# Last products of a half projection and first weights of the gated unit, reordered in a two-layer decoder trunk

## The chip, the core and the metric

The kernel runs on one core of a Trainium2 chip. The metric is the time of one execution on the device in microseconds (us): the median of several runs. The engines are named as in the profile: PE is TensorE (matrix products), DVE is VectorE, ACT is ScalarE, POOL is GpSimd, and SP is SyncE, whose queue issues the DMA transfers.

## What is computed

Two layers over 1024 tokens of width 1024, in float32: an attention layer, then a state-space (S5) layer whose output is gated. Cut to the part that the change touches (the second layer, `h` being the normed input):

```python
proj = h @ w_in                                   # 1024 x 2048
u, z = proj[..., :1024], proj[..., 1024:]
y = s5_scan(u, ...)                               # per group of 16 channels
g = gelu(y)
y = g * sigmoid(g @ w_glu + b_glu)                # the gated unit
x = x + rms_norm((y * silu(z)) @ w_out, post_norm)
```

## The kernel before

**Products.** Every float32 matrix is split in two reduced-precision parts, a high part (the cast) and a low part (what the cast left out), so that one product becomes three: high weights with high input, high weights with low input, low weights with high input. `proj_half` (L119) makes one *half projection*: 128 output channels for 512 tokens, which is 8 steps k of 128 input channels, 3 products each, 24 products of 128x512 into one PSUM bank. `proj_part` (L107) issues them, k by k, in the order hi·hi, hi·lo, lo·hi, so that the low part of the weights is wanted by the third product.

**Weights.** `load_w` (L95) fetches one 128x1024 block of weights by DMA from SP (L100, tile `wraw`), ACT casts it (L88, `whi`), and DVE subtracts (L89, `wlo`). The pools of all three have two buffers, so the load of block e+2 waits until block e is split, and the split of block e+2 until PE is done with block e.

**The second layer.** `layer1` runs 16 blocks of `ssm_w_in` through `in_order` (L774), each for both token halves (th 0 and 1). The first 8 give `u`, the last 8 give `z` (L1463 on ACT, L1464 on DVE, stored to `z_dr`). Between these projections the state-space work for 8 groups of channels runs: products `py` on PE (L1433, L1434), a gelu that goes ACT L1435 and L1436, POOL L1437 and L1438, ACT L1439, DVE L1440, and a store of the rows `Y` to DRAM (`y_dr`, L1441), in two halves per group.

**The gated unit.** `glu` (L1494) reads `y_dr` back transposed (SP L1506, tile `gy`, six half-tile slots in a ring), for th 0 and 1 and for 8 k each, and splits each piece: ACT casts it (L88, `g0b` for th 0, `g1b` for th 1) and DVE takes the low part (L89). A slot is refilled when its piece has been split. `in_order` with `start="block"` then runs the first four half projections (two blocks of weights, two token halves; PSUM tiles `psb`) together: first k 0 to 6 of all four, then the four triples of k 7, whose input comes last from the last group. After these, blocks 2 to 7 follow one half after the other (`psj`). The output projection (`pso`, weights `wf0h`, `wf1b`) stands behind.

**The order.** Each engine runs its own instructions strictly in the order in which a scheduler has put them when the kernel is built; the scheduler estimates times of its own, and `high_priority` (in `load_w`) and `issue_after` shift what it picks. An instruction that waits holds up all that stands behind it on its engine.

Of the kernel before, what the change touches and what calls it, by code (L numbers as in the profile page):

```python
# [23 lines left out]
P = 128  # L24
S = 1024
D = 1024
KT = 8
# [18 lines left out]
def f32(ap):  # L46
    return ap.bitcast(F32)
# [36 lines left out]
def split(c, hi, lo, src, scale=None, engine=None):  # L84

    nc = c.nc
    if scale is None:
        c.last_hi = nc.scalar.copy(hi, src).ins  # L88
        return (engine or nc.vector).tensor_tensor(lo, src, f32(hi), op=ALU.subtract)  # L89
    else:  # L90
        nc.scalar.activation(hi, src, AF.Copy, scale=scale)
        nc.vector.scalar_tensor_tensor(lo, src, scale, f32(hi), op0=ALU.mult, op1=ALU.subtract)


def load_w(c, src):  # L95

    nc = c.nc
    with c.tc.high_priority(AHEAD):
        raw = c.wraw.tile([P, KT * P], F32, tag="wraw", name="wraw")
        nc.sync.dma_start(raw, src)  # L100
        hi = c.wsp.tile([P, KT * P], F32R, tag="whi", name="whi")
        lo = c.wsp.tile([P, KT * P], F32R, tag="wlo", name="wlo")
        c.last_lo = split(c, hi, lo, raw, engine=c.w_engine).ins
    return hi, lo


def proj_part(c, ps, w, h, ks, first=True):  # L107

    nc = c.nc
    wh, wl = w  # L110
    hh, hl = h
    for k in ks:
        s = slice(k * P, k * P + P)
        for n, (a, b) in enumerate(((wh, hh), (wh, hl), (wl, hh))):
            nc.tensor.matmul(ps, a[:, s], b[:, k, :], start=first and k == 0 and n == 0,  # L115
                             stop=k == KT - 1 and n == 2, skip_group_check=True)


def proj_half(c, w, h):  # L119
# [861 lines left out]
def post_weight(c, src):  # L981

    t = c.outs.tile([P, D], F32, tag="O", name="post", bufs=4)
    c.nc.sync.dma_start(t, bass.AP(src.tensor, src.offset, [[0, P], [1, D]]))
    return t
# [458 lines left out]
def y_view(c, et, th):  # L1444

    return bass.AP(c.y_dr.tensor, c.y_dr.offset + et * P * S + th * 4 * 16384, [[P, P], [16384, 4], [1, P]])
# [44 lines left out]
    return groups[7].load_U.ins  # L1491


def glu(c, a, last_input):  # L1494
    nc, tc = c.nc, c.tc
    bh = c.cst.tile([P, KT], F32, name="bh")
    nc.sync.dma_start(bh, a["b_glu"])
    nc.vector.tensor_scalar(bh, bh, 0.5, None, op0=ALU.mult)
    g, y2 = [], []
    ring = [x[:, n * H:n * H + H] for x in (c.outs.tile([P, D], F32, tag="O", name="gy", bufs=4) for _ in range(3)) for n in range(2)]  # L1500
    for th, tags in enumerate((("b1", "b4"), ("b5", "b3"))):
        g.append([c.pb.tile([P, KT, H], F32R, tag=t, name=f"g{th}{t}") for t in tags])
        for et in range(8):
            y = ring[(8 * th + et) % 6]
            with tc.issue_after(last_input):
                nc.sync.dma_start(y.rearrange("p (i n) -> p i n", i=4), y_view(c, et, th))  # L1506
            split(c, g[th][0][:, et, :], g[th][1][:, et, :], y)
    y2.append([c.pb.tile([P, KT, H], F32R, tag=t, name=f"y0{t}") for t in ("b0", "b2")])

    def use(eo, th, ps):  # L1510
        if th == 1 and len(y2) == 1:
            y2.append([c.pa2.tile([P, KT, H], F32R, tag=t, name=f"y1{t}") for t in ("y1h", "y1l")])
        t, z, y = c.slot("tg"), c.slot("zg"), c.slot("yg")
        nc.sync.dma_start(z, c.z_dr[eo, :, th * H:th * H + H])
        nc.sync.dma_start(y.rearrange("p (i n) -> p i n", i=4), y_view(c, eo, th))
        nc.gpsimd.tensor_tensor(z, z, y, op=ALU.mult)
        with tc.high_priority(AHEAD):
            nc.scalar.activation(t, ps, AF.Tanh, scale=0.5, bias=bh[:, eo:eo + 1])
            nc.vector.scalar_tensor_tensor(z, t, 1.0, z, op0=ALU.add, op1=ALU.mult)
            split(c, y2[th][0][:, eo, :], y2[th][1][:, eo, :], z, 0.25)  # L1520

    in_order(c, [a["w_glu"][e] for e in range(8)], g, use, start="block")
    return y2


def trunk(tc, a):
    c = Ctx()
    nc = tc.nc
    c.nc, c.tc = nc, tc
    c.turn = 0  # L1530

    c.banks, c.wide = 0, 0
    with ExitStack() as es:
        pool = lambda name, **k: es.enter_context(tc.tile_pool(name=name, **k))
        c.cst = pool("cst", bufs=1)
        c.small = pool("small", bufs=3)
        c.wraw = pool("wraw", bufs=2)
        c.wsp = pool("wsp", bufs=2)
        c.ring = pool("ring", bufs=1)
        c.outs = pool("outs", bufs=1)  # L1540
        c.psj = pool("psj", bufs=2, space=PSUM)
        c.pst = pool("pst", bufs=2, space=PSUM)
        c.pso = pool("pso", bufs=2, space=PSUM)

        c.es_ps = es.enter_context(ExitStack())
        c.ps = lambda name, bufs: c.es_ps.enter_context(tc.tile_pool(name=name, bufs=bufs, space=PSUM, reuse_waits="tile"))
        c.psl = c.ps("psl", 2)
        c.dr = pool("dr", bufs=1, space=DRAM)
        dram = lambda name, shape: c.dr.tile(shape, F32, name=name)
        c.vec_dr = dram("vec_dr", [3, 16, 384])  # L1550
        c.v_dr = dram("v_dr", [3, 2, S, H])
        c.ms_dr = dram("ms_dr", [8, 3, 4, S])
        c.wt_dr = dram("wt_dr", [8, 3, 2, S])
        c.on_dr = dram("on_dr", [8, P, S])
        c.x1_dr = dram("x1_dr", [8, P, D])
        c.g_dr = dram("g_dr", [8, P, S])
        c.u_dr = dram("u_dr", [8, P, S])
        c.y_dr = dram("y_dr", [8, P, S])
        c.z_dr = dram("z_dr", [8, P, S])
        c.k_dr = dram("k_dr", [64, 16, 240])  # L1560
        c.ca_dr = dram("ca_dr", [8, P, 1152])
        c.bt_dr = dram("bt_dr", [8, P, S])
        c.tab_dr = dram("tab_dr", [P, S + H])
        c.rot_dr = dram("rot_dr", [8, 3, 64, S])
        c.identr = c.cst.tile([P, P], F32R, name="identr")
        c.ident = f32(c.identr)
        tabs = c.cst.tile([P, 11, 2, 32], F32, name="tabs")
        pairs = [(tabs[:, k, 0, :], tabs[:, k, 1, :]) for k in range(11)]
        c.apow, c.bfac, c.rot = pairs[0:3], pairs[3], pairs[4:11]
        c.rho = c.cst.tile([P, 64], F32, name="rho")  # L1570
        c.dsk = c.cst.tile([P, 8], F32, name="dsk")

        c.es_pa = es.enter_context(ExitStack())
        c.pa = c.es_pa.enter_context(tc.tile_pool(name="pa", bufs=1, side="left"))
        c.es_attn = es.enter_context(ExitStack())
        h = attention(c, a)
        c.es_attn.close()
        c.es_ps.close()
        c.psl = c.ps("psl2", 2)
        c.pb = es.enter_context(tc.tile_pool(name="pb", bufs=1, side="right", reuse_waits="tile"))  # L1580
        g, raw = attn_gate(c, a, h)
        z112 = c.outs.tile([P, D], F32, tag="O", name="z112", bufs=4)[:, 0:8 * 112]
        nc.gpsimd.memset(z112, 0.0)
        nc.sync.dma_start(bass.AP(c.k_dr.tensor, c.k_dr.offset, [[8 * 240, P], [240, 8], [1, 112]]),
                          z112.rearrange("p (k x) -> p k x", k=8))
        h1, ws = attn_out(c, a, g, raw)
        c.es_pa.close()
        last_input = layer1(c, a, h1, ws)
        c.es_pa.close()
        c.pa2 = c.es_pa.enter_context(tc.tile_pool(name="pa2", bufs=1, side="left", reuse_waits="tile"))  # L1590
        y2 = glu(c, a, last_input)

        w = [[c.pa2.tile([P, KT, H], F32R, tag=f"w0{x}", name=f"wf0{x}") for x in "hl"],
             [c.pb.tile([P, KT, H], F32R, tag=t, name=f"wf1{t}") for t in ("b1", "b4")]]
        for n in range(2):
            for k in range(KT):
                rw = c.wraw.tile([P, H], F32, tag="wraw", name="wfr")
                nc.sync.dma_start(rw, a["ssm_w_out"][k, :, n * H:n * H + H])
                split(c, w[n][0][:, k, :], w[n][1][:, k, :], rw)
        post = post_weight(c, a["ssm_post_norm"])  # L1600
        ov = a["out"].rearrange("(n i) d -> i n d", i=8)
        out_tiles(c, y2, w, post, lambda i: c.x1_dr[i], lambda i, x: nc.sync.dma_start(ov[i], x), K_ORDER, 1,
                  lambda x, ns: nc.sync.dma_start(ov[7][:, ns], x[:, ns]))
# [90 lines left out]
```

## Time and profile before

| what | before |
|---|---|
| time, median of 3 runs (lowest to highest) | 1668.17 us (1667.24 to 1670.62) |
| the profiled execution, its time | 1668.29 us |
| the profiled execution, its span | 1666.5 us |
| PE busy | 1640.4 us, 98% |
| DVE, ACT, POOL busy | 1020.5, 709.6, 469.7 us |

The span counts from the first instruction to the last; some 1.8 us of the measured time lie around it. PE is the engine to read: where it is busy without a break at its full clock, other engines can only matter by keeping it so. The table of waits shows which of its idle stretches were ended by what, the timeline gives the single instructions, and PEclk (1.00 is 2.4 GHz, 0.50 is 1.2 GHz) tells how fast a busy PE ran.

### The profile page before, as it was taken

To read this page: it belongs to the slowest core of one execution; us is meant where nothing else is said; L and a number is where in the kernel's file an instruction comes from. 1 tells how busy PE (TensorE), PEld (TensorE's weight loads), DVE (VectorE), ACT (ScalarE), POOL (GpSimd) and SP (SyncE) were. 2 spreads that over 40 slices of the span, in tenths; PEclk is the share of its full clock that TensorE was granted. 3 is DMA by queue.
4 is the path that set the end of the run, shared out by engine and by line. 5 is a ranking of instruction groups with operands and counts; after the bars stand their busy time and mean duration, and the time that the engine had idled before them with its cause. 6 is when DMAs were issued, how large, how long until landed. Compare 5 with 4: busy or idle time off the path is not lost.

```text
span 1666.5 us, 26394 instructions
## 1 busy us (share of the span) xinstructions
PE 1640.4 (98%) x9746; PEld 1389.8 (83%) x9746; DVE 1020.5 (61%) x2513; ACT 709.6 (43%) x1732; POOL 469.7 (28%) x303
## 2 busy tenths in 40 slices
PE   7999999999999999999999999999999999899998
PEld 5889999988888888888888888888888888777886
DVE  8698898725455454545545454557563799945533
ACT  5232222326556454655646464555353232334411
POOL 2000010141342522434252243503320455522121
PEclk8999999999999999999999999999999999999999
DMA  6223455441232323323232332416336888574522
GB/s 227 87 50 108 154 170 175 136 146 55 70 102 72 110 74 91 93 72 99 72 109 87 92 105 76 133 52 192 125 115 206 246 247 239 170 225 156 167 103 87
DMA packets 176858, 212.21 MB, mean 127 GB/s; under 512 B 37443, under 2 KB 133462, under 8 KB 176728
## 3 DMA queue, kind: packets, MB, share of 16 engines
q1 hardware_dynamic: 176728, 210.52, 42.0%
q8 instruction: 77, 1.26, 0.3%
q14 instruction: 53, 0.43, 0.1%
HBM read 153.51 MB, written 56.96 MB: 126 GB/s over the span
## 4 chain that ended last, share of the span: by engine, by line
PE 88%; DVE 6%; DMA 3%; issue 1%; POOL 1%; ACT 1%; SPq 0%; DVEq 0%; ACTq 0%; POOLq 0%
PE psj L115 47%; PE psq L378 10%; PE psl L476 5%; PE pso L553 4%; PE pt L504 4%; PE pso L897 3%; PE pso L899 3%; PE pso L898 3%; PE pso L579 1%; PE psb L115 1%; PE psv L239 1%; PE psv L238 1%; DVE wlo L89 1%; PE psv L237 1%; DVE T L1414 1%
## 5 line engine op out<-in xcount | busy, mean ns | idle before, releaser
L115 PE MATMUL psj<-hh,wlo 128*128 128x512 f32 x896 | 358.3, 400 | 0.0
L115 PE MATMUL psj<-hh,whi 128*128 128x512 f32 x896 | 358.2, 400 | 0.0
L115 PE MATMUL psj<-hl,whi 128*128 128x512 f32 x896 | 354.9, 396 | 0.0
L89 POOL TENSOR_TENSOR wlo<-wraw,whi 128x1024 fp32r<-128x1024 f32 x48 | 115.3, 2402 | 392.6 <-ACT whi L88 347.3
L115 PEld LDWEIGHTS psj<-hh,whi 128*128 128x128 f32 x896 | 168.9, 188 | 36.6
L115 PEld LDWEIGHTS psj<-hh,wlo 128*128 128x128 f32 x896 | 168.8, 188 | 36.5
L115 PEld LDWEIGHTS psj<-hl,whi 128*128 128x128 f32 x896 | 168.9, 188 | 36.0
L493 ACT ACTIVATE lg<-lg,nm 128x128 f32<-128x128 f32 (+1 forms) x384 | 168.2, 443 | 35.5 <-DVE nm L488 35.5
L482 DVE CUSTOM_DVE_ANT_0 lg<-psl,T 128x128 f32<-128x128 f32 (+1 forms) x384 | 110.6, 347 | 90.4 <-PE psl L476 90.4
L88 ACT CAST whi<-wraw 128x1024 fp32r<-128x1024 f32 x80 | 83.7, 1046 | 131.9 <-PE psj L115 87.1
L378 PE MATMUL psq<-whi,v 128*128 128x256 f32 x640 | 115.6, 280 | 0.0
L115 PE MATMUL psj<-h1h,wlo 128*128 128x512 f32 (+1 forms) x272 | 103.9, 383 | 4.6 <-DVE wlo L89 4.6
L89 DVE TENSOR_TENSOR ph<-pt,ph 128x512 fp32r<-128x512 f32 (+2 forms) x160 | 96.7, 622 | 15.6 <-ACT ph L88 13.5
L89 DVE TENSOR_TENSOR kl<-psj,kh 128x512 fp32r<-128x512 f32 x48 | 33.2, 692 | 117.8 <-ACT kh L88 117.3
L115 PE MATMUL psj<-h1h,whi 128*128 128x512 f32 (+1 forms) x272 | 105.2, 387 | 0.0
L115 PE MATMUL psj<-h1l,whi 128*128 128x512 f32 (+1 forms) x272 | 103.0, 379 | 0.2 <-DVE h1l L89 0.2
L88 ACT CAST ph<-pt 128x512 fp32r<-128x512 f32 (+2 forms) x160 | 81.6, 530 | 46.3 <-PE pt L504 45.3
L378 PEld LDWEIGHTS psq<-whi,v 128*128 128x128 f32 x640 | 98.4, 188 | 1.2 <-ACT whi L88 0.6
L378 PE MATMUL psq<-wlo,v 128*128 128x256 f32 x320 | 89.8, 281 | 1.2 <-DVE wlo L89 1.2
L553 PE MATMUL pso<-ph,vs 128*128 128x256 f32 (+1 forms) x544 | 86.5, 284 | 0.0
L1277 POOL TENSOR_TENSOR Ks<-Ks,O 128x16 f32<-128x16 f32 x8 | 4.0, 498 | 285.4 <-ACT Ks L1275 285.4
L504 PE MATMUL pt<-identr,lg 128*128 128x128 f32 x560 | 82.2, 276 | 0.0
(288 smaller groups left out, 3719.6 us busy)
## 6 DMA issues: line engine op xcount, KB each, us to landing
wraw<-in_w_in_dram SPq DMA_DIRECT2D x56, 512.0 KB
mw<-wt_dr SPq DMA_DIRECT2D x48, 256.0 KB
v<-in_w_v_dram SPq DMA_DIRECT2D x20, 512.0 KB
vp<-v_dr SPq DMA_DIRECT2D x16, 512.0 KB
wraw<-in_ssm_w_in_dram SPq DMA_DIRECT2D x16, 512.0 KB
v_dr<-v SPq DMA_DIRECT2D x30, 256.0 KB
rot_dr<-rt SPq DMA_DIRECT2D x48, 128.0 KB
ca_dr<-ca SPq DMA_DIRECT2D x32, 144.0 KB
```

Of the source, the lines that this page charges most:

```text
L88: c.last_hi = nc.scalar.copy(hi, src).ins
L89: return (engine or nc.vector).tensor_tensor(lo, src, f32(hi), op=ALU.subtract)
L115: nc.tensor.matmul(ps, a[:, s], b[:, k, :], start=first and k == 0 and n == 0, stop=k == KT - 1 and n == 2, skip_group_check=True)
L378: nc.tensor.matmul(o, r[x][:, k, ts], w[y][:, k, :], skip_group_check=True, start=i in (0, 4, 5) and t % 2 == k == n == 0, stop=k == 3 and ...
L476: nc.tensor.matmul(psl[:, h, o], x[HEADS[h], qs], y[HEADS[h], ks], start=j == js[0] and n == 0, stop=n == 2, skip_group_check=True)
L482: nc.vector.tensor_tensor_reduce(lg[:, h, j, 0:w], psl[:, h, o], bt[:, h, 256 - w:256], scale=1.0, scalar=-3.0e38, op0=ALU.add, op1=ALU.ma ...
L493: nc.scalar.activation(lg[:, h, j, 0:w], lg[:, h, j, 0:w], AF.Exp, bias=nm[:, h, b:b + 1], accum_out=ms[:, col:col + 1])
L504: c.nc.tensor.transpose(pt[:, n * P:(n + 1) * P], lg[:, h, j, part * P:part * P + P], c.ident)
L553: nc.tensor.matmul(o, l, r, start=n == 0, stop=n == len(jobs) - 1, skip_group_check=True)
L897: nc.tensor.matmul(ps, gh[:, k, ts], wh[:, k, cols], start=n == 0, stop=False)
L898: nc.tensor.matmul(ps, gh[:, k, ts], wl[:, k, cols], start=False, stop=False)
L899: nc.tensor.matmul(ps, gl[:, k, ts], wh[:, k, cols], start=False, stop=n == KT - 1)
```

## The change

Two edits, neither of which adds or removes an instruction.

First, a flag `low_last`, set once attention is over. With it `proj_part` issues the sixteen products with high weights first and the eight with low weights behind them, within what it is given: all 24 of a half projection, or, in the block at the start of the gated unit, the k 0 to 6 (14 and 7) and the k 7 apart.

Second, in `glu`, the first block of `w_glu` is loaded and split after the pieces of th 0 and two pieces (`FIRST_W = 2`) of th 1; the splits of the other pieces of th 1 may be issued only behind that block's cast and its low part. The second block is loaded behind all of them. Both are handed to `in_order` as `ws`, which before loaded them itself.

```diff
 def proj_part(c, ps, w, h, ks, first=True):
-    nc = c.nc
-    wh, wl = w
-    hh, hl = h
-    for k in ks:
-        s = slice(k * P, k * P + P)
-        for n, (a, b) in enumerate(((wh, hh), (wh, hl), (wl, hh))):
-            nc.tensor.matmul(ps, a[:, s], b[:, k, :], start=first and k == 0 and n == 0,
-                             stop=k == KT - 1 and n == 2, skip_group_check=True)
+    nc = c.nc
+    order = [(k, n) for k in ks for n in range(3)]
+    if c.low_last:
+        order.sort(key=lambda x: x[1] == 2)
+    for m, (k, n) in enumerate(order):
+        nc.tensor.matmul(ps, w[n == 2][:, k * P:k * P + P], h[n == 1][:, k, :], start=first and k == 0 and m == 0,
+                         stop=m == len(order) - 1 and k == KT - 1, skip_group_check=True)
...
+FIRST_W = 2
...
 def glu(c, a, last_input):
+    ws, behind = [], []
     for th, tags in enumerate((("b1", "b4"), ("b5", "b3"))):
         g.append([c.pb.tile([P, KT, H], F32R, tag=t, name=f"g{th}{t}") for t in tags])
         for et in range(8):
+
+            if th == 1 and et == FIRST_W:
+                ws.append(load_w(c, a["w_glu"][0]))
+                behind = [c.last_hi, c.last_lo]
             y = ring[(8 * th + et) % 6]
             with tc.issue_after(last_input):
                 nc.sync.dma_start(y.rearrange("p (i n) -> p i n", i=4), y_view(c, et, th))
-            split(c, g[th][0][:, et, :], g[th][1][:, et, :], y)
+            with ExitStack() as es:
+                for i in behind:
+                    es.enter_context(tc.issue_after(i))
+                split(c, g[th][0][:, et, :], g[th][1][:, et, :], y)
+    ws.append(load_w(c, a["w_glu"][1]))
...
-    in_order(c, [a["w_glu"][e] for e in range(8)], g, use, start="block")
+    in_order(c, [a["w_glu"][e] for e in range(8)], g, use, start="block", ws=ws)
...
+    c.low_last = False
...
         c.pb = es.enter_context(tc.tile_pool(name="pb", bufs=1, side="right", reuse_waits="tile"))
+        c.low_last = True
         g, raw = attn_gate(c, a, h)
```

What the scheduler makes of it, at three places. On PE, the last block of `ssm_w_in` for th 0 (PSUM tile `psj_14825`, weights `whi_14792` and `wlo_14793`), before:

```order
L115 MATMUL psj_14825<-h1h0_12335,whi_14792 128x512 [waits DVE_49,Activation_49]
L115 MATMUL psj_14825<-h1l0_12336,whi_14792 128x512
L115 MATMUL psj_14825<-h1h0_12335,wlo_14793 128x512 [waits DVE_49]
L115 MATMUL psj_14825<-h1h0_12335,whi_14792 128x512
L115 MATMUL psj_14825<-h1l0_12336,whi_14792 128x512
```

and of the change (its last three products with high weights, and what follows):

```order
L115 MATMUL psj_14825<-h1l0_12336,whi_14792 128x512
L115 MATMUL psj_14825<-h1h0_12335,whi_14792 128x512
L115 MATMUL psj_14825<-h1l0_12336,whi_14792 128x512
L115 MATMUL psj_14825<-h1h0_12335,wlo_14793 128x512 [waits DVE_49]
L115 MATMUL psj_14825<-h1h0_12335,wlo_14793 128x512 x7
```

The wait for the low part moved from the third product to the seventeenth. On ACT, around the casts of the first two blocks of `w_glu` (before `whi_15014` and `whi_15020`, of the change `whi_14994` and `whi_15018`; `g1b5` is th 1's high part, `Y2` the gelu of the last group), before:

```order
L1439 ACTIVATE Y2_14855<-Y2_14855 128x512 [waits Pool_49]
L88 CAST g1b5_14984<-gy_14957 128x512 [waits DMAHW1_49]
L1439 ACTIVATE Y2_14873<-Y2_14873 128x512 [waits Pool_49]
L88 CAST g1b5_14984<-gy_14957 128x512 [waits DMAHW3_49]
L88 CAST whi_15014<-wraw_15012 128x1024 [waits PE_49]
L1463 ACTIVATE z1_14915<-psj_14890 128x512 [waits PE_49]
L88 CAST g1b5_14984<-gy_14955 128x512 [waits DMAHW5_49]
```

and of the change:

```order
L1439 ACTIVATE Y2_14855<-Y2_14855 128x512 [waits Pool_49]
L1439 ACTIVATE Y2_14873<-Y2_14873 128x512 [waits Pool_49]
L88 CAST whi_14994<-wraw_14992 128x1024 [waits PE_49]
L88 CAST g1b5_14984<-gy_14957 128x512 [waits DMAHW1_49]
L88 CAST g1b5_14984<-gy_14957 128x512 [waits DMAHW3_49]
L1463 ACTIVATE z1_14915<-psj_14890 128x512 [waits PE_49]
L88 CAST g1b5_14984<-gy_14955 128x512 [waits DMAHW5_49]
```

The weights' cast and the second L1439 moved ahead of two casts of th 1's pieces. Some ten rows further up, one more pair changed places: a cast of `g0b` (k 5) now stands ahead of the second L1439 of the group before the last, and not behind it. On PE, in the block, at the last of the pieces that come by the ring (th 1, k 5; `psb_15026` is block 0 and th 1, `psb_15027` block 1 and th 1), before:

```order
L115 MATMUL psb_15026<-g1b5_14984,whi_15014 128x512 [waits Activation_49]
L115 MATMUL psb_15026<-g1b3_14985,whi_15014 128x512 [waits DVE_49]
L115 MATMUL psb_15026<-g1b5_14984,wlo_15015 128x512
L115 MATMUL psb_15026<-g1b5_14984,whi_15014 128x512
L115 MATMUL psb_15026<-g1b3_14985,whi_15014 128x512
L115 MATMUL psb_15026<-g1b5_14984,wlo_15015 128x512
L115 MATMUL psb_15027<-g1b5_14984,whi_15020 128x512
```

and of the change:

```order
L115 MATMUL psb_15026<-g1b5_14984,whi_14994 128x512 [waits Activation_49]
L115 MATMUL psb_15027<-g1b5_14984,whi_15018 128x512
L115 MATMUL psb_15026<-g1b3_14985,whi_14994 128x512 [waits DVE_49]
L115 MATMUL psb_15026<-g1b5_14984,whi_14994 128x512
L115 MATMUL psb_15026<-g1b3_14985,whi_14994 128x512
L115 MATMUL psb_15026<-g1b5_14984,wlo_14995 128x512 x7
```

In the order before, 57 of the block's 96 products stand ahead of the first row here and 38 behind it; in that of the change 52 stand ahead and 43 behind. The order of SP's transfers around this place is the same in both.

## Rows read from the trace of the kernel before

**Rows 1.** The page: busy time, share of the span and instructions by engine.

```profile
PE 1640.4 (98%) x9746; PEld 1389.8 (83%) x9746; DVE 1020.5 (61%) x2513; ACT 709.6 (43%) x1732; POOL 469.7 (28%) x303
```

**Rows 2.** Waits of PE, 40 to 1666 us: engine, line, waited for, total us, times, longest.

```profile
PE psj L115 <- DVE wlo L89: 4.6, 1, 4.6
PE psb L115 <- ACT whi L88: 1.8, 1, 1.8
PE psq L378 <- DVE wlo L89: 1.5, 2, 1.2
```

**Rows 3.** Timeline of PE at the stall: start us, duration us, instruction, [idle before].

```profile
1451.46 0.39 PE L115 MATMUL psj<-h1h,whi 128*128 128x512 f32 x1
1451.69 0.39 PE L115 MATMUL psj<-h1l,whi 128*128 128x512 f32 x1
1456.64 0.80 PE L115 MATMUL psj<-h1h,wlo 128*128 128x512 f32 x1 [4.56 <-DVE wlo L89]
```

**Rows 4.** Timeline of DVE, just ahead of that stall's end.

```profile
1454.96 1.62 DVE L89 TENSOR_TENSOR wlo<-wraw,whi 128x1024 fp32r<-128x1024 f32 x1
```

**Rows 5.** Timeline of PE, the start and the end of the block.

```profile
1477.50 0.40 PE L115 MATMUL psj<-h1h,wlo 128*128 128x512 f32 x1
1479.74 1.03 PE L115 MATMUL psb<-g0b,whi 128*128 128x512 f32 x2 [1.85 <-ACT whi L88]
...
1503.19 0.40 PE L115 MATMUL psb<-g1b,wlo 128*128 128x512 f32 x1
1503.93 0.73 PE L115 MATMUL psj<-g0b,whi 128*128 128x512 f32 x2 [0.34 <-ACT whi L88]
```

**Rows 6.** Windows: us, busy PE, PEld, DVE, ACT, POOL (count), PEclk, DMA share, GB/s.

```profile
194.10:196.00 1.90, 1.89 (x16) 1.89 (x17) 1.90 (x4) 0.00 (x0) 0.00 (x0) 1.00 0.35 101
1456.00:1459.00 3.00, 2.36 (x6) 1.88 (x7) 2.27 (x3) 0.00 (x0) 1.73 (x1) 0.52 0.41 83
1479.70:1483.00 3.30, 3.25 (x8) 2.57 (x9) 3.27 (x5) 2.96 (x5) 0.00 (x0) 0.54 0.61 169
1484.00:1488.00 4.00, 4.00 (x19) 3.30 (x18) 0.56 (x2) 0.62 (x1) 0.00 (x0) 1.00 1.12 326
1515.00:1658.00 143.00, 143.00 (x646) 117.94 (x645) 60.73 (x131) 39.03 (x75) 33.86 (x25) 1.00 0.39 129
```

**Rows 7.** Timeline of ACT, 1474 to 1494 us.

```profile
1474.87 0.62 ACT L1439 ACTIVATE Y<-Y 128x512 f32<-128x512 f32 x1
1478.13 0.62 ACT L88 CAST g1b<-gy 128x512 fp32r<-128x512 f32 x1 [2.64 <-DMA gy<-y_dr]
1478.65 1.04 ACT L88 CAST whi<-wraw 128x1024 fp32r<-128x1024 f32 x1
...
1487.27 0.62 ACT L88 CAST g0b<-gy 128x512 fp32r<-128x512 f32 x1 [4.61 <-DMA gy<-y_dr]
...
1492.93 0.62 ACT L88 CAST g1b<-gy 128x512 fp32r<-128x512 f32 x1 [3.59 <-DMA gy<-y_dr]
```

**Rows 8.** Timeline of POOL, the last group's second half.

```profile
1472.16 1.61 POOL L1438 TENSOR_TENSOR Y<-Y,Y 128x512 f32<-128x512 f32 x1
```

**Rows 9.** Timeline of SP, DMA issues (no idle times): 1476 to 1489 us.

```profile
1476.31 0.33 SPq L1441 DMA_DIRECT2D y_dr<-Y  x1
...
1480.98 0.33 SPq L100 DMA_DIRECT2D wraw<-in_w_glu_dram  x1
1481.79 0.37 SPq L1506 DMA_DIRECT2D gy<-y_dr  x1
...
1488.64 0.37 SPq L1506 DMA_DIRECT2D gy<-y_dr  x1
```

**Rows 10.** Timeline of DVE: the last piece's low part.

```profile
1493.58 0.69 DVE L89 TENSOR_TENSOR g1b<-gy,g1b 128x512 fp32r<-128x512 f32 x1 [3.52 <-ACT g1b L88]
```

**Rows 11.** Timeline of ACT: the last cast of the output weights.

```profile
1580.10 0.62 ACT L88 CAST wf1b<-wfr 128x512 fp32r<-128x512 f32 x1 [0.95 <-DMA wfr<-in_ssm_w_out_dram]
```

**Rows 12.** Timeline of PE: the first product with them, k 0.

```profile
1579.96 0.39 PE L897 MATMUL pso<-wf1b,y0b 128*128 128x512 f32 x1
```

## Prediction

> **What bounds the kernel now.** I read the busy shares first: PE works 98% of the span [rows 1], so time can only come out of PE's pauses and its slow stretches. The table of waits then says which pauses a reader should look for in code that the change touches. From 40 us on there are few: 4.6 us for a low part of weights in the second layer's projection, 1.8 us for a high part at the start of the gated unit's block, and 1.5 us in two waits in the attention layer's own products, which are not reordered [rows 2]. The timeline of PE puts the first at 1452 to 1456.64 us, behind two products of the last block of weights [rows 3], and the second at 1477.9 to 1479.74 [rows 5]. The windows show what each pause costs beyond itself: behind the first PE ran at a granted clock of 0.52, behind the second at 0.54, both mostly at the lower of its two levels (1.2 GHz), and at 1.00 again before 1484 [rows 6]. Of 2.36 us of work at 0.52 some 1.1 are lost, of 3.25 us at 0.54 some 1.5. So the two places hold 4.6 + 1.1 + 1.8 + 1.5 = 9.0 us, and no more is there to be won. From 1515 to 1658 PE is busy 143.00 of 143.00 us at full clock [rows 6]: what is won or lost before passes through to the end, if the output weights stay ahead.
>
> **The first edit: low products last.** In every half projection after the attention layer the wait for the low part moves from product 3 to product 17. Everywhere but at one place nothing waits there now, so reordering is worth nothing: the same 24 products at the same 0.23 us each [rows 3]. The one place is the last block of weights for th 0. DVE delivers its low part at 1454.96 + 1.62 = 1456.58 [rows 4], and the change leaves what DVE does ahead of it in place, so this end stays. PE now has 14 more products in hand: 14 x 0.23 = 3.2 us of work fill the pause, which shrinks from 4.56 to 1.3 us. Whether the clock falls for 1.3 us is bounded by two rows: behind the attention layer's wait of 1.2 us the clock was 1.00, behind the 1.85 us it was 0.54 [rows 2, 5, 6]. 1.3 lies nearer to the first, so I take it that the clock holds. PE is then through with the projection not at 1477.90 (1477.50 + 0.40, [rows 5]) but 3.2 + 1.1 = 4.3 us earlier, at 1473.6; with the fall, at 1474.7.
>
> **The second edit: the weights' cast moves up on ACT.** What ends the second pause is the cast of the first block, and the row shows why it was late: it took 1.04 us from 1478.65, behind a cast of a th 1 piece that had waited 2.64 us for its DMA [rows 7]. That one is now behind it. But the cast cannot go when PE would like it: it stands behind the second L1439 of the last group, which waits for POOL's L1438, and this ended at 1472.16 + 1.61 = 1473.77 [rows 8]. This chain is not shortened by the change. It is even fed a little later: the pair that changed places further up puts one cast, 0.62 us at most [rows 7], ahead of the group before's L1439, whose DVE step stands ahead of the splits that free the slots; I take 0.3, bounds 0 and 0.6. So: L1439 at 1474.1 (now 1474.87, because of the casts between), some 0.55 to the next start, the weights' cast 1474.6 to 1475.7, and the block starts at 1475.7 where it started at 1479.74: 4.0 us earlier, bounds 3.7 and 4.3. PE, ready at 1473.6, waits 2.1 us for it. This is longer than the 1.85 us behind which the clock fell, so I charge the same 1.5 us at its start. The first edit's gain is thereby mostly turned into a wait at the next place, and whether the clock held at the first does not matter: with the fall PE comes at 1474.7 and still waits.
>
> What is queued behind the moved cast: on ACT two casts of th 1 pieces, the z activation L1463 and the second block's cast; on DVE the low part of the weights now stands ahead of these pieces' low parts. PE wants the pieces only after 42 products, 10 us later, and the second block after 21 products, near 1482; its cast stands behind the piece that DMA lets go at 1478.13 [rows 7] and three more instructions, which start some 0.52 us apart as that cast and the next do: 1478.65 + 1.6 + 1.04 = 1481.3, so it comes in time by 0.7. I take nothing for these.
>
> **What is late next: the last piece of th 1.** The block still needs the piece of k 5, the last to come through the ring. Its slot is freed by the split of th 0's k 7, and that piece by the store that L1440 lets go at 1476.31. The row chain reads: store issued 1476.31, piece k 7 requested 1481.79, cast 1487.27, k 5 requested 1488.64, cast 1492.93 [rows 7, 9], low part done at 1493.58 + 0.69 = 1494.27 [rows 10]. In the old order PE reached it at about 1494.5, having 57 products ahead of it, so it was just in time. In the new order 52 products stand ahead: from 1475.7, 52 x 0.23 = 12.0, and 1.5 for the clock, PE wants it at 1489.2. The chain comes earlier by 0.8, as L1439 does. A second gain is possible: SP held the load of the third block of weights until 1480.98 [rows 9], when the first was split; the DMA engines were busy only 0.61 of 1479.7 to 1483 [rows 6], so 0.39 x 3.3 = 1.3 us were left unused, just before the two pieces were asked for. Now that load goes at about 1477. Bounds: the cast of k 5 stays at 1492.9, or comes 0.8 + 1.3 = 2.1 us earlier, at 1490.8. I take 1490.8, since SP's order is the same and the load moves wholly into the idle share. Then its low part is there 1.34 us later (the same rows), at 1492.1, and 42 products follow: 42 x 0.23 = 9.7, end at 1501.8. But PE has stood for some 2.2 us, more than the 1.85, and I charge 1.5 again: 1503.3. Today its last product starts at 1503.19 [rows 5], so the block ends at 1503.4. **Change: 0.1 us.** Without the clock's fall it is -1.6; with the cast at 1492.9 it is +2.0.
>
> Here a rule of the Trainium skill speaks for the early bound: "DMA: Bandwidth & Descriptors", Queues, rings and completion order, says that each DMA engine takes the descriptors of one queue's ring in order. By it the load issued earlier is out of the pieces' way and the sum is the 0.1 above; if transfers shared evenly, the earlier load would slow the store of 1476.31 as well, and the sum would be the +2.0. No row here tells the two apart, and the numbers above stand without it.
>
> **Behind the block.** The split of the output weights must stay ahead: the last of their eight casts is at 1580.10, the first product with them at 1579.96 [rows 11, 12]. That cast is k 7; in the 24-product groups each k is worth three products, so PE reaches it 7 x 3 x 0.23 = 4.8 us later at the earliest. A shift of up to 4 us would be covered, and mine is 0.1.
>
> **How the numbers follow.** The profiled execution took 1668.29 us (span 1666.5), 0.12 over the median of 1668.17; the difference is below what I can size. What a measurement can tell from no change is about 0.2%, 3.3 us.
>
> Forecast: both waits shift, the end stays: 1668.17 - 0.1 = 1668.0; its own range, from the bounds, is 1666.5 to 1670.2. Chance 0.60.
>
> Rival 1, the last piece is in time: if its cast comes before 1488.6 (a further 2.2 us, which both shortened requests would have to share), the block runs through from 1475.7 for the old 23.7 us: end 1499.4, -4.0, 1664.2. For it speaks that both transfers, 5.5 and 4.3 us from request to cast [rows 7, 9], ran into full DMA engines (1.12 in 1484 to 1488, [rows 6]); against it, that the bytes are the same. Chance 0.15.
>
> Rival 2, both pauses and both slow stretches vanish: the block starts at 1473.6 and its 96 products take 96 x 0.23 = 22.1, end 1495.7, -7.7, 1660.5. It needs POOL's chain to come 2.1 us earlier and the last piece 5; nothing in the rows offers that. Chance 0.08.
>
> Rival 3, slower: the earlier load of 512 KB gets ahead of the store or the k 7 piece. At the 326 GB/s of a full stretch [rows 6] this is 1.6 us: k 5's cast at 1492.9 + 1.6 = 1494.5, low part 1495.9, end 1495.9 + 9.7 + 1.5 = 1507.1, +3.7, 1671.9. It counts as slower from a cast at 1494.1 on. Chance 0.13.
>
> Rival 4, the order matters nowhere, because the pauses are ended by something that the rows don't name: no change, 1668.2. Chance 0.04.
>
> The chance of faster is rivals 1 and 2, 0.23; slower rival 3 and a tail of the forecast, 0.14; within, 0.63. The range leaves out rival 2, a few hundredths below rival 1, and half of rival 3: 1663.0 to 1671.5.
>
> **What would show it.** In the changed profile: a pause of 1.3 us on PE before the first low product near 1456.6, with PEclk near 1.00 behind it; `psb` starting near 1475.7 behind the cast of weights; a new wait of PE `psb` for ACT `g1b` or DVE near 1489 to 1492, with a lower PEclk after it; the block's end near 1503. It is wrong if no such new wait shows (rival 1), if POOL's L1438 ends well before 1473.5 (rival 2), or if k 7's cast comes later than 1487.3 (rival 3).

## The result

The changed kernel takes 1672.62 us (median of 11 runs, 1669.9 to 1674.4) against 1668.4 us of the kernel before on the same chips. The ratio is 1.0022, with a 95% interval of 1.0014 to 1.0030: slower by 3.7 us, 2.3 to 5.0 (the two medians lie 4.2 apart). The forecast was 1668.0 us and no change, with a range up to 1671.5. Its third rival, slower by 3.7 us because a load of weights gets in the way of a late piece of input, had been given 0.13.

The profiled execution of the changed kernel took 1674.40 us, its span is 1672.5. On the page the busy times moved little [rows 1]:

```profile
PE 1643.2 (98%) x9746; PEld 1391.7 (83%) x9746; DVE 1026.1 (61%) x2513; ACT 710.3 (42%) x1732; POOL 467.7 (28%) x303
```

The table of PE's waits, 1440 to 1515 us, answers [rows 2]. The wait for the low part shrank from 4.6 to 2.1 us, the one for the weights' cast is still 1.8 us in two pieces, and a new one stands first:

```profile
PE psb L115 <- ACT g1b L88: 3.8, 1, 3.8
PE psj L115 <- DVE wlo L89: 2.1, 1, 2.1
PE psb L115 <- ACT whi L88: 1.8, 2, 1.1
PE psj L115 <- ACT whi L88: 0.3, 1, 0.3
```

Executions of any of these kernels differ by some us in code that no version here touches, so positions must be compared from a mark behind it. The mark is the first product of the state-space layer (L1407), the end the last product of the output (L899). One execution each of before, of the changed kernel, and a second of either (e9, e10), in this order; the columns of a group's row are the shortest, median and longest time in ns, then the first and last start in us:

```profile
L1407 PE MATMUL pv<-U,BT x128: 273/275/275, 1296.5 to 1431.3; 128*128 128x128 f32 x128
L899 PE MATMUL pso<-wf1b,y1y1l x40: 281/394/394, 1620.2 to 1658.5; 128*128 128x512 f32 x24, 128*128 128x256 f32 x16
```

```profile
L1407 PE MATMUL pv<-U,BT x128: 271/275/275, 1299.7 to 1434.4; 128*128 128x128 f32 x128
L899 PE MATMUL pso<-wf1b,y1y1l x40: 281/394/394, 1626.2 to 1664.5; 128*128 128x512 f32 x24, 128*128 128x256 f32 x16
```

```profile
L1407 PE MATMUL pv<-U,BT x128: 273/275/275, 1300.8 to 1435.5; 128*128 128x128 f32 x128
L899 PE MATMUL pso<-wf1b,y1y1l x40: 281/394/394, 1623.0 to 1661.2; 128*128 128x512 f32 x24, 128*128 128x256 f32 x16
```

```profile
L1407 PE MATMUL pv<-U,BT x128: 271/275/275, 1296.9 to 1431.6; 128*128 128x128 f32 x128
L899 PE MATMUL pso<-wf1b,y1y1l x40: 281/394/394, 1622.9 to 1661.2; 128*128 128x512 f32 x24, 128*128 128x256 f32 x16
```

The mark lies anywhere from 1296.5 to 1300.8 us, whichever kernel runs. From mark to end before takes 362.0 and 360.4 us, the changed kernel 364.8 and 364.3: 2.3 to 4.4 us more, which covers the 3.7 of the runs. So the loss lies behind the mark. Ahead of it, from the first logits product of attention (L476) on, the two first profiles take 935.4 and 935.2 us. Positions in the changed profile stand 3.2 us late against [rows 3 to 10] by the mark (1299.7 - 1296.5); below, "moved back" means less 3.2.

The block of the gated unit, on PE's timeline (start, duration, idle before), answers [rows 5]:

```profile
1460.54 2.86 PE L115 MATMUL psj<-h1h,wlo 128*128 128x512 f32 x8 [2.13 <-DVE wlo L89]
1479.97 3.48 PE L115 MATMUL psb<-g0b,whi 128*128 128x512 f32 x14 [1.15 <-ACT whi L88]
...
1485.75 3.49 PE L115 MATMUL psb<-g0b,whi 128*128 128x512 f32 x14 [0.69 <-ACT whi L88]
...
1496.98 2.50 PE L115 MATMUL psb<-g1b,whi 128*128 128x512 f32 x5 [3.85 <-ACT g1b L88]
...
1509.54 0.40 PE L115 MATMUL psb<-g1b,wlo 128*128 128x512 f32 x1
```

Moved back, the block starts at 1476.8 where it started at 1479.74, 3 us earlier, and ends at 1506.3 where it ended at 1503.2, 3 us later. Between the two PE stands 0.69 us for the weights of the second block and 3.85 us for the piece k 5 of th 1. The windows (us, busy PE and so on, PEclk, DMA share) show that it then works at half clock, 1.2 GHz, and a little more:

```profile
1488.00:1491.00 3.00, 3.00 (x15) 2.46 (x14) 1.03 (x2) 1.24 (x2) 0.00 (x0) 1.00 0.93 279
...
1497.00:1500.00 3.00, 3.00 (x7) 2.38 (x8) 0.65 (x1) 0.00 (x0) 2.88 (x2) 0.50 0.19 63
1500.00:1503.00 3.00, 3.00 (x9) 2.31 (x9) 0.00 (x0) 0.00 (x0) 0.03 (x1) 0.57 0.27 82
```

Fifteen products fall into a stretch of 3 us at full clock, 7 and 9 here. At clocks of 0.50 and 0.57, 3.00 x 0.50 + 3.00 x 0.43 = 2.8 us are lost behind the wait.

### The profile page after: what moved, and what is told of

The parts are those of the page before. It is cut to its first block, busy times and chain, and to the rows that moved or that the text cites. A ratio compares the mean times of both kernels' runs of the same rounds, so it can differ in the third digit from the quotient of the medians.

```text
span 1672.5 us, 26389 instructions
## 1 busy us (share of the span) xinstructions
PE 1643.2 (98%) x9746; PEld 1391.7 (83%) x9746; DVE 1026.1 (61%) x2513; ACT 710.3 (42%) x1732; POOL 467.7 (28%) x303
## 4 chain that ended last, share of the span: by engine, by line
PE 84%; DVE 8%; DMA 4%; issue 2%; POOL 1%; ACT 1%; SPq 0%; DVEq 0%; ACTq 0%; POOLq 0%
PE psj L115 45%; PE psq L378 10%; PE psl L476 5%; PE pso L553 4%; PE pt L504 4%; PE pso L897 3%; PE pso L899 3%; PE pso L898 3%; PE pso L579 1%; DVE T L1414 1%; DMA gy<-y_dr 1%; DVE T L1419 1%; PE psv L239 1%; PE psv L238 1%; PE psb L115 1%
## 5 line engine op out<-in xcount | busy, mean ns | idle before, releaser
L115 PE MATMUL psj<-hh,wlo 128*128 128x512 f32 x896 | 349.8, 400 | 0.0
L88 ACT CAST whi<-v 128x1024 fp32r<-128x1024 f32 x35 | 36.8, 1051 | 104.6 <-PE psq L378 82.9
```

The costliest lines, as they stand in the source:

```text
L115: nc.tensor.matmul(ps, w[n == 2][:, k * P:k * P + P], h[n == 1][:, k, :], start=first and k == 0 and m == 0, stop=m == len(order) - 1 and ...
```

## The experiments

Each ran against the kernel before; "mark to end" is from one profile of each, read as above. Interval in brackets. The kernel before was run again beside them, with medians of 1668.4 to 1669.4 us, so the ratios compare, and the medians of two rows only roughly.

| run | what | median us | ratio to before | mark to end |
|---|---|---|---|---|
| change | both edits | 1672.62 | 1.0022 [1.0014, 1.0030] | 364.8 |
| e1 | first edit alone | 1673.91 | 1.0025 [1.0013, 1.0036] | 365.8 |
| e2 | second edit alone | 1668.12 | 0.9997 [0.9988, 1.0006] | 360.0 |
| e3 | both, block k by k | 1671.53 | 1.0013 [1.0004, 1.0022] | 364.1 |
| e4 | both, fourth weights' load later | 1671.38 | 1.0012 [1.0003, 1.0021] | 363.1 |
| e5 | both, ring swapped | 1667.57 | 0.9988 [0.9979, 0.9997] | 360.2 |
| e6 | both, tanh first | 1671.58 | 1.0019 [1.0009, 1.0028] | 363.8 |
| e7 | before, ring swapped | 1669.05 | 1.0001 [0.9992, 1.0010] | 359.3 |
| e8 | both, ring swapped, tanh first | 1667.69 | 0.9995 [0.9986, 1.0004] | 358.9 |
| e11 | first edit, ring swapped | 1667.86 | 0.9994 [0.9984, 1.0003] | 360.7 |
| e12 | second edit, ring swapped | 1668.81 | 0.9997 [0.9988, 1.0005] | 359.2 |

**Which edit.** e1 leaves `glu` as it was, e2 leaves the flag off:

```diff
# e1
-            if th == 1 and et == FIRST_W:
+            if th == 9:
...
-    ws.append(load_w(c, a["w_glu"][1]))
# e2
-        c.low_last = True
+        c.low_last = False
```

> Only the first edit (low products last); the weights of the gated unit are split in the old order. Theory A (the last piece of th 1, k 5, comes late because its DMA stands behind others, and PE now reaches it earlier): the weights' cast is as late as before, the block starts near the old place, PE reaches k 5 after 52 products in place of 57 and waits about 1 us for it: 0 to 1.5 us over before, 1668.4 to 1670. Theory B (the first edit itself is the cost, since it reorders VectorE in the projection so that the last low part comes 0.7 us later and everything hangs on that): as slow as the whole change, 1671.5 to 1673. Theory C (the extra time lies in the attention layer, which the change doesn't touch): no change against before from the state-space products on.

> Only the second edit (first weights of the gated unit split earlier). The 4.6 us pause for the low part stays. Theory A: the block starts about 1.5 us earlier than before, the piece k 5 has 57 products ahead of it, so PE meets it at its old time or up to 1 us earlier; the transfer for it is hindered as in the whole change: -1.0 to +1.0 us, 1667.4 to 1669.4. Theory B (first edit is the cost): the same as before or faster by up to 1.5 us. Theory D (the second edit is the cost, by the moved cast and the earlier loads): 1671 to 1673.

The first edit alone is as slow as both, the second alone as fast as before. That is theory B's answer by the numbers; what of the first edit costs was still open. Theory C is out: in e1 the time is lost behind the mark. In e1 the waits name the same place as in the changed kernel:

```profile
PE psb L115 <- ACT g1b L88: 4.1, 1, 4.1
PE psb L115 <- ACT whi L88: 3.0, 1, 3.0
PE psj L115 <- DVE wlo L89: 2.0, 1, 2.0
```

Theory A had said about 1 us for the first of them and was wrong in size. With the first edit PE comes to the block earlier and to k 5 after fewer products, and the piece does not come earlier: the first edit makes the wait. But e1 is not the first edit with all else as before. In its order on ACT the cast of the first block's weights stands right behind the second L1439, ahead of one of the two pieces of th 1 that the second edit moves behind it:

```profile
1476.21 1.03 ACT L88 CAST whi<-wraw 128x1024 fp32r<-128x1024 f32 x1
```

That is 179.4 us behind the mark; the changed kernel has 179.2, the two profiles of before 182.2 and 180.7. Theory A's condition that the cast is as late as before did not hold, and e1 has most of what the second edit does at this place. In e2, where PE comes late, its waits in the block are 0.2 us for ACT and 0.2 for DVE, though k 5 takes 6.3 us from request to cast there.

**The order within the block.** e3 turns the flag off inside the block, and PE's order alone moves:

```diff
+                keep, c.low_last = c.low_last, False
                 proj_part(c, ps, ws[e], h[th], ks)
+                c.low_last = keep
```

> The whole change, but in the block of the gated unit the products go k by k as before (low products last only in whole half projections); the orders of the other engines are those of the whole change. Theory A: PE has 57 products ahead of k 5 and 38 behind it; the wait for it shrinks by some 1 us, 0.9 us fewer products follow, so the block ends 0.9 us earlier: 1671.7 against 1672.6. If instead the order of products within the block makes the loss: 1668.5 to 1669.5.

1671.53, 1.1 us under the change (1.5 by the ratios); its wait for k 5 is 2.4 us. Theory A's 0.9 us fits, and the rival's 3 to 4 does not. The intervals of e3 and the change overlap, so the times do not show that the five more products ahead of the piece help; only the shorter wait in one profile speaks for it.

**What k 5 stands behind.** SP asks for k 5 once th 0's k 7 has been split, since it takes that slot. In the changed profile SP's issues, ACT's casts (with their wait), were:

```profile
1485.41 1.26 SPq L1515 DMA_DIRECT2D gy<-y_dr  x2
...
1488.26 0.69 SPq L100 DMA_DIRECT2D wraw<-in_w_glu_dram  x1
1489.05 0.43 SPq L1465 DMA_DIRECT2D z_dr<-z  x1
1489.93 0.37 SPq L1515 DMA_DIRECT2D gy<-y_dr  x1
```

```profile
1488.56 0.62 ACT L88 CAST g0b<-gy 128x512 fp32r<-128x512 f32 x1 [2.37 <-DMA gy<-y_dr]
...
1496.31 0.62 ACT L88 CAST g1b<-gy 128x512 fp32r<-128x512 f32 x1 [5.68 <-DMA gy<-y_dr]
```

Against [rows 7, 9] the k 7 piece took 3.2 us from request to cast in place of 5.5. The load of the third block was issued 4.2 us ahead of it and not 0.8, which was the forecast's reason; it is not all of it, since in e5 below the distance is the same and k 7 took 4.9. But k 5 took 6.4 in place of 4.3, being asked for 1.7 us behind the 512 KB of the fourth block of weights, where before 4.4 us lay between the two issues (second profile of the change: 2.3 us, and 5.4 from request to cast). The load in the profile of before:

```profile
1484.25 1.97 SPq L100 DMA_DIRECT2D wraw<-in_w_glu_dram  x1
```

The same two distances can be read in all eight profiles that have this ring and this load ahead of k 5 (before, e9, the change, e10, e1, e2, e3, e6). The load was issued 4.4 to 1.2 us ahead of k 5's request, and the cast came 4.3 to 7.2 us behind the request, longer the nearer the load was; from the load's issue to the cast it was 7.7 to 8.7 us every time. The load itself stands behind k 7's request in SP's queue, 2.5 to 3.5 us later. So a k 7 that lands earlier brings the request for k 5 nearer to the load, and k 5 hardly earlier. e4 issues that load behind k 5 and moves nothing else:

```diff
+            if start == "block" and e == 3:
+                es.enter_context(c.tc.issue_after(c.last_gy))
             w = load_w(c, srcs[e])
```

> The whole change, but SP issues the load of the fourth block of gated-unit weights (512 KB) behind the request for piece k 5 and not ahead of it; nothing else moves. Theory A (k 5 queues behind that load in the DMA engines): request to cast shrinks from 6.4 us to 4.3 to 4.8 us, PE's wait from 3.9 to about 2 us: 1670.5 to 1671. Rival (transfers share the engines, or the landing hangs on something else): 6.0 to 6.4 us again and 1672.6.

```profile
1486.26 0.37 SPq L1518 DMA_DIRECT2D gy<-y_dr  x1
1486.68 0.66 SPq L100 DMA_DIRECT2D wraw<-in_w_glu_dram  x1
```

```profile
1490.95 0.62 ACT L88 CAST g1b<-gy 128x512 fp32r<-128x512 f32 x1 [3.93 <-DMA gy<-y_dr]
```

4.7 us from request to cast and 2.1 us of wait, within what theory A gave; the time, 1671.38, lies 0.4 above it, and its interval overlaps that of the change. So, by these profiles, the load in front costs k 5 0.7 to 1.7 us, and the rest of the wait is there without it. The Trainium skill, "DMA: Bandwidth & Descriptors", Queues, rings and completion order, says that an engine takes a ring's descriptors in order; these rows agree, and the same rule that favoured the change at k 7 speaks against it at k 5.

**Taking the wait away.** e5 lets k 5 use another slot, one that is free early, and gives the slot behind k 7 to th 1's k 7, which only the last six products of the block read:

```diff
-            y = ring[(8 * th + et) % 6]
+            y = ring[{13: 3, 15: 1}.get(8 * th + et, (8 * th + et) % 6)]
```

> The whole change, with two pieces of th 1 swapped in the ring of slots: k 5 takes the slot that k 1 of th 1 frees early, and k 7 of th 1, which only the block's last six products use, takes the slot behind k 7 of th 0. Theory A (all of the loss is PE's wait for k 5 and the slow clock behind it): the wait of 3.9 us and some 1.5 us of slow clock vanish, nothing else moves: 5 us less than the whole change, 1667 to 1668, so as fast as before or faster by 1 us. Rival (the first edit costs by PE's other waits, the slow clock at the block's start, and a later chain through ScalarE): 1670 to 1672.

> The kernel before, with the same swap of two pieces in the ring. There PE meets k 5 without a wait, so by theory A nothing is won: 1668.4, within 0.5. If the swap by itself makes the block faster (fewer transfers in the way of k 7): 1667 or less.

The changed kernel with the swap takes 1667.57: 5.0 us less than the change (5.7 by the ratios), as theory A said, and 0.9988 [0.9979, 0.9997] of before, the one version here whose interval lies under 1. The same swap in the kernel before is worth nothing (1.0001). That the loss is gone is clear. That it has become a gain is barely so: the interval ends 0.0003 under 1, e8 below with the same edits and the same swap cannot be told from before, and from mark to end e5's profile takes only 0.2 us less than the second one of before (360.2 and 360.4). The wait for k 5 is gone from PE's table, and the pause at the block's start is all that is left of the block's waits:

```profile
PE psb L115 <- ACT whi L88: 2.7, 1, 2.7
PE psj L115 <- DVE wlo L89: 2.0, 1, 2.0
PE psj L115 <- ACT whi L88: 0.3, 1, 0.3
```

Its block, and the windows that show what the pause costs beyond itself:

```profile
1478.65 6.33 PE L115 MATMUL psb<-g0b,whi 128*128 128x512 f32 x14 [2.69 <-ACT whi L88]
```

```profile
1478.60:1482.00 3.40, 3.35 (x8) 2.68 (x9) 2.64 (x5) 1.64 (x3) 0.00 (x0) 0.50 1.11 353
1482.00:1485.00 3.00, 3.00 (x9) 2.32 (x8) 2.47 (x4) 2.45 (x4) 0.00 (x0) 0.53 1.10 371
```

This is where the first edit's gain goes even with k 5 out of the way: PE comes early, waits 2.7 us for the weights' cast, and runs the first 14 products in 6.3 us in place of 3.5.

**The two edits once more, with the swap.**

> The first edit alone (low products last), with the two pieces of th 1 swapped in the ring. Theory A (the first edit lost only by the wait for k 5): the 4.1 us wait and its slow clock vanish: 5 us under the first edit alone, 1668.5 to 1669.5, as fast as before. If the first edit has another cost: 1671 or more.

> The second edit alone (first weights split earlier), with the swap in the ring. Without the first edit PE met k 5 nearly in time, so the swap should bring little: 1667.5 to 1668.5, 0 to 0.6 us under the second edit alone. If it is as fast as or faster than the whole change with the swap (1667.6), the first edit adds nothing even with the wait for k 5 gone.

The first edit goes from 1.0025 to 0.9994 by the swap (6 us in the medians, 5.2 by the ratios; 5 were expected), the second stays at 0.9997. With k 5 out of the way neither edit alone can be told from before, and both together win 0.5 to 3.5 us by e5's interval, which overlaps those of e11 and e12.

**The chain through ScalarE.** e6 puts the exchanged pair back, the tanh L1439 of the group before the last ahead of a cast; e8 does that with the swap:

```diff
+        c.gelu = nc.scalar.activation(T2, T2, AF.Tanh, scale=2.0 * math.sqrt(2.0 / math.pi)).ins
+        if et == 6:
+            c.gelu6 = c.gelu
...
-                for i in behind:
+                for i in behind + [c.gelu6] * (th == 0 and et >= 5):
```

> The whole change, with one pair on ScalarE put back: the gelu's tanh (L1439) of the group before the last runs ahead of the cast of piece k 5 of th 0, as before the change. If that pair delays the chain to the last store by its 0.5 to 0.8 us: the last weights' cast and the k 5 piece come 0.5 to 1.2 us earlier, 1671.5 to 1672 against 1672.6. If the delay of the chain has another source (the last low part in the projection ends 0.7 us later, on VectorE beside GpSimd): no change, 1672.6.

> The whole change with both repairs, the swap in the ring and the tanh ahead of the cast. Theory A: the swap's 5 us and up to 0.8 us for an earlier weights' cast at the block's start: 1666.2 to 1667.5, faster than before by 1 to 2 us. Rival (the first edit costs elsewhere): 1670 to 1672.

e6 is 1.0 us under the change and e8 0.1 over e5 (0.5 and 1.2 by the ratios); both differences are inside the intervals, and e8 does not reach the 1666.2 to 1667.5 expected. In e6's profile the block starts 0.7 us earlier by the mark, at 179.5 in place of 180.3, and the wait for k 5 is 4.0 us, no shorter. In e8's the pause at the block's start is 0.24 us, and one of 2.25 us stands at the second block's weights. So the pair delays the weights' cast, but the last piece does not come the sooner without it; what it costs in time stays open.

**The two kernels once more.**

> The kernel before once more, for a second profile. The executions differ by some us in the attention layer's first 300 us, in every kernel; the question is how far the rest differs. If the profile shown is typical, from the first state-space product to the last product takes 362.0 us again, within 0.5, with both pauses (4.6 and 1.8 us). If its block was a slow one: 359.5 to 361, with the second pause shorter.

> The changed kernel once more, for a second profile. Theory A (PE's wait for the piece k 5 with the slow clock behind it is the loss in every execution): a wait of 3 to 4.5 us for it again, and 364.8 us from the first state-space product to the last product, within 1.

e10 has the wait for k 5 again, 3.1 us, and 364.3 us from mark to end: the loss is not an accident of one execution. e9 shows that the second pause of before was one. Its waits from 1440 to 1515 us:

```profile
PE psj L115 <- DVE wlo L89: 4.5, 1, 4.5
PE psb L115 <- ACT g1b L88: 0.4, 1, 0.4
PE psj L115 <- ACT whi L88: 0.3, 1, 0.3
PE psb L115 <- DVE g1b L89: 0.2, 1, 0.2
```

No wait for the weights' cast. The reason is on its ACT timeline:

```profile
1480.89 0.62 ACT L88 CAST g1b<-gy 128x512 fp32r<-128x512 f32 x1 [1.83 <-DMA gy<-y_dr]
1481.41 1.04 ACT L88 CAST whi<-wraw 128x1024 fp32r<-128x1024 f32 x1
```

The cast that had held it up at 1478.13 [rows 7], 181.6 us behind the mark, comes 180.1 behind it here, and the weights' cast with it. The second edit shortens a pause that one of two executions did not have (nor had that of e7); with that goes that e2 wins nothing that can be measured.

## Why the prediction was wrong

**The pause for the low part: right in kind, too short.** Forecast 1.3 us, measured 2.1 (2.0 to 2.2 in all runs with the first edit). Its start was right: 1460.54 - 2.13 - 3.2 = 1455.2, where 16 products from 1451.46 end. Its end was not: the low part came at 1460.48 - 3.2 = 1457.3 and not at 1456.58. "The change leaves what DVE does ahead of it in place" was not true of the order (the step L1464 now stands behind the four scans L1414 and not ahead of them), though the subtraction starts as before, at 1458.20 - 3.2 = 1455.0 where it started at 1454.96. What changed is how long it took:

```profile
1458.20 2.28 DVE L89 TENSOR_TENSOR wlo<-wraw,whi 128x1024 fp32r<-128x1024 f32 x1
```

```profile
1457.83 1.57 POOL L1438 TENSOR_TENSOR Y<-Y,Y 128x512 f32<-128x512 f32 x1
```

The same subtraction took 1.62 us before [rows 4] and 2.28 here, next to a GpSimd instruction that had begun 0.37 us earlier. The Trainium skill, "SBUF — State Buffer", SBUF: two separate sides, says that a VectorE operation with two SBUF inputs and a GpSimd operation that reads SBUF lock each other out, the first to start going first. The row is near to that: 1457.83 + 1.57 + 1.22 (the time of such a subtraction at 1482.67 of the profile before, with no GpSimd work near) would end at 1460.62, the measured end is 1460.48. In the profile of before GpSimd's pair L1437 and L1438 came 1.0 us later, and the subtraction, from 1454.96 on, met the shorter first one:

```profile
1454.58 0.94 POOL L1437 TENSOR_SCALAR Y<-Y 128x512 f32<-128x512 f32 x1
```

The same sum gives 1454.58 + 0.94 + 1.22 = 1456.74 there, where 1456.58 was measured. This is no accident of one execution: the subtraction took 1.62 or 1.63 us in all five profiles without the first edit and 2.28 or 2.29 in all nine with it. All that hangs on the buffer which this frees, the second weights' load and the two requests behind it, started 0.7 us later.

Nor did the clock hold, as I had taken it to: it was 0.73 and 0.66 in the two stretches behind this pause (the last rows of this document), which costs 0.27 x 2.5 + 0.34 x 3.0 = 1.7 us. PE was through with the projection at 1476.83 + 1.99 - 3.2 = 1475.6 and not at 1473.6.

**The block's start: 3.0 us earlier, not 4.0.** The cast stood behind L1439 and this behind POOL's L1438, as forecast; that ended at 1476.72 + 1.60 - 3.2 = 1475.1, 1.3 us later than in [rows 8]. I had taken 0.3 for the exchanged pair, and nothing for the low part that came late.

```profile
1476.72 1.60 POOL L1438 TENSOR_TENSOR Y<-Y,Y 128x512 f32<-128x512 f32 x1
```

ACT's rows further up show both terms, the late pieces and the pair:

```profile
1466.21 0.62 ACT L88 CAST g0b<-gy 128x512 fp32r<-128x512 f32 x1 [8.83 <-DMA gy<-y_dr]
1467.03 0.62 ACT L88 CAST g0b<-gy 128x512 fp32r<-128x512 f32 x1 [0.20 <-DMA gy<-y_dr]
1467.56 0.63 ACT L1439 ACTIVATE Y<-Y 128x512 f32<-128x512 f32 x1
```

The first cast and L1439 stood at 1462.38 and 1462.91 in the profile of before. Moved back, the cast is 0.6 us later and L1439 1.4: the pair took 0.8 us, above my bound of 0.6.

PE, itself late, waited 1.15 us for the cast and not 2.1, and the slow clock that I had charged with 1.5 us at the block's start did not follow:

```profile
1480.00:1483.00 3.00, 3.00 (x13) 2.50 (x14) 2.35 (x4) 1.56 (x3) 0.00 (x0) 1.00 1.11 362
```

The second block's weights, which I had in time by 0.7 us, came 0.7 late. These errors partly cancel: PE reached k 5 at 1496.98 - 3.85 - 3.2 = 1489.9, where I had 1489.2.

**The last piece: the step that failed.** "The chain comes earlier by 0.8, as L1439 does" and "I take 1490.8": the second L1439 came at 1478.36 - 3.2 = 1475.2, 0.3 later than in [rows 7], and k 5's cast at 1496.31 - 3.2 = 1493.1, beyond even the late bound of 1492.9. The 1.3 us of unused transfer time that I credited were won, at k 7 (a transfer 2.3 us shorter), and lost again at k 5 (2.1 us longer), which I had charged with the time it had taken in [rows 7, 9], though the change moved the load in front of it nearer. The fourth block's load follows k 7's request in SP's queue, and k 5's cast came 8.0 us behind the issue of that load, as it had come 8.7 behind it before: what k 7 won could not be passed on. The working from there was sound but for one term: hi and lo from such a cast, 42 products and a slow clock give 1493.1 + 1.3 + 9.7 + 1.5 = 1505.6 for the block's end; it was 1506.3 + 0.2, the clock's fall having cost 2.8 us and not 1.5 (in e10, by its clocks of 0.68 and 0.71, 1.7).

**The base.** The gain was set against a pause of 1.85 us that the second profile of before does not show. Against that profile the block of the changed kernel starts not 3.0 but 1.7 us earlier (180.3 and 182.0 us behind the mark), and ends 4.6 later. One term of the chain differs there that I had left as it was: from the store of the last rows to k 7's request it took 5.5 us in the first profile of before [rows 9] and 3.8 in the second, 5.3 and 6.2 in the two of the change. Why is open.

**The rivals.** Rival 3 had the sign, the size and the kind of cause, a load of 512 KB ahead of a late piece, but its place was the store or k 7; it was k 5, and the load the fourth block's and not the third's. That its 3.7 us is the measured figure is luck: its own sign, a cast of k 7 later than 1487.3, did not come (1488.56 - 3.2 = 1485.4), its k 5 was cast at 1494.5 where 1493.1 was measured, and the clock's fall cost more than its 1.5 us. Rival 1, the piece in time, is what e5 made, and there the time fell to 1667.6, not to 1664.2: the old 23.7 us of the block that it counted on contained the slow clock of one short pause, and the pause was longer. That the output weights stay ahead held: from the block's end to the last product is 155.0 us in the changed profile and 155.3 before.

## What to carry to other kernels

Work that is moved ahead to fill one wait only brings forward the moment at which the next input is wanted; follow each input of the next stage back to the request of its transfer, and to the buffer slot that holds this request up, before counting the gain. A slot rotation fixes which piece comes last: giving the late slot to the piece that is read last took away a loss of 3.7 us and left a gain of some 2, barely clear of the noise. A transfer that is asked for behind a large load on the same queue may not gain from being asked for earlier. Before building a gain on a pause that a DMA ends, look at a second execution of the same program.

## What the runs showed of the hardware

A pause's length alone did not tell whether TensorE's clock would fall. Behind 1.85 us of idle PE it was 0.54 [rows 5, 6]; in e5, behind 2.0 us in front of the low products, it stayed at 1.00:

```profile
1459.20:1463.00 3.80, 3.73 (x24) 3.38 (x25) 1.21 (x3) 0.00 (x0) 0.00 (x0) 1.00 0.64 185
```

and in the changed kernel, behind 2.13 us at the same place, PE began its low products at full clock and was slowed only among them:

```profile
1460.50:1463.00 2.50, 2.46 (x8) 2.02 (x9) 1.18 (x2) 0.00 (x0) 0.00 (x0) 0.73 0.38 79
1463.00:1466.00 3.00, 3.00 (x19) 2.91 (x19) 0.00 (x0) 0.00 (x0) 0.00 (x0) 0.66 1.05 354
```

The cost of a fall differed as much: some 1.5 us behind the 1.85 of before, 2.8 us behind the 2.69 of e5, and in front of the same product, 2.8 us behind the 3.85 of the change and 1.7 behind the 3.12 of e10. And the time from the start of an execution to the mark differs by 4 us between executions of one program, in code with the same instructions in the same order, which is as much as the change was worth.
